# Second norm of a transformer block: products on GpSimd, full value on ScalarE, and the last output tiles one by one

## The chip, the cores and the metric

One Trainium2 chip, of which the kernel uses one core. A core has TensorE (PE: matmuls; PEld is its weight loads), VectorE (DVE), ScalarE (ACT), GpSimd (POOL) and SyncE (SP), which issues the DMAs. The engines run their own instruction lists in order and wait for each other by semaphores. The metric is the device time of one execution in microseconds (us).

## The reference

A block of width 1024 over 256 tokens in float32: an adaLN modulation from a vector c, a norm, one wide projection, causal attention of 8 heads beside a spatial gating unit, a merge, an output projection, and then the part that matters here: a second norm and a feed-forward layer of width 4096, each with a residual, and a final norm.

```python
h = rmsnorm(x, g_ffn[l]) * (1 + scale2) + shift2
x = x + gate2 * (jnp.square(jax.nn.relu(h @ w_ff1[l])) @ w_ff2[l])
return rmsnorm(x, g_final)
```

with `rmsnorm(x, g) = x * rsqrt(mean(x*x) + EPS) * g`.

## The kernel before

Everything is held transposed, features on the 128 partitions and the 256 tokens along a row, so a 1024 x 256 activation is eight tiles (ft 0 to 7) of 128 x 256. Each float32 product is made of three matmuls (`mm3`, line 70): a weight tile is rounded by ScalarE to a high part (`whi`, `high`, line 240) and VectorE forms the rest (`wlo`, `low`, line 249); an activation has a high part (`nh`, `fh`) and a low part (`nl`, `fl`) in the same way; high x high, high x low and low x high are added up in PSUM.

The feed-forward layer runs over 16 units of 256 hidden features. For units 0 to 2 the first product (`ff1`, line 619) works on the unnormalised x, so that TensorE need not wait for the norm; the roots of the second norm are multiplied in afterwards (`relu2`, line 630). From unit 3 on the product is `wide` (line 404) with the normalised activation `nh`, `nl`, which `full` (line 653) makes once for all eight tiles, tile by tile: x times the roots (`xb`, line 657), the rounded high part `nh` (line 658), the full value in place of the product (line 659), and the difference `nl` (line 660). `xb` comes from a pool tag with two buffers, so the product of tile ft writes the buffer of tile ft - 2 and waits until the `nl` of that tile has been read out of it. `full` is called for tiles 0 and 1, then 2 to 4, then 5 to 7 (lines 704, 708, 717). `ff2` (line 674) adds each unit's second product into four PSUM banks, two tiles to a bank.

PE, DVE and ACT are wrapped by `InOrder` (line 35): in the first and in the last part of the program instructions keep the order of the code, and from line 369 to line 728 a scheduler sets the order of each engine's list before the kernel runs. All instructions of the three wrapped engines carry line 44, so they are told apart by the tiles they write and read. GpSimd's instructions keep their own lines.

In the last part (lines 730 to 778) the last two units' second products are made for two tiles at a time (j = 0 to 3). VectorE adds the residual from PSUM (`x_sb`, line 740), ScalarE squares it (`sq3`, `sqt`), VectorE and once GpSimd (line 749) add the squares, and `yg` is x times the gain of the final norm. `turn` (line 758) transposes `yg` on TensorE, `sums` (line 118) adds the squares over the features with matmuls against ones, `rstd` (line 123) makes the roots on ScalarE (`ms`) and GpSimd (`rs`), and ScalarE and VectorE scale the result (`ys`) for four output DMAs.

Of the kernel before, what the change touches and what calls it, by code (L numbers as in the profile page):

```python
# [9 lines left out]
F32 = mybir.dt.float32  # L10
F32R = mybir.dt.float32r
BF16 = mybir.dt.bfloat16
AF = mybir.ActivationFunctionType
ALU = mybir.AluOpType
AX = mybir.AxisListType

P = 128
S = 256
D = 1024
KT = D // P  # L20
# [4 lines left out]
NU = DFF // 256  # L25
# [4 lines left out]
G_MIX, G_FFN, G_FIN, G_SGU = 48, 56, 64, 72  # L30
# [17 lines left out]
def block_kernel(ctx, tc, x, xT, cols, wsguT, bsgu, w_a1, w_1, w_a, w_m, w_f, out):  # L48
    nc = tc.nc
    PE, DVE, ACT = (InOrder(tc, e) for e in (nc.tensor, nc.vector, nc.scalar))  # L50
    const = ctx.enter_context(tc.tile_pool(name="const", bufs=1))
    act = ctx.enter_context(tc.tile_pool(name="act", bufs=1))
    wk = ctx.enter_context(tc.tile_pool(name="wk", bufs=2))
# [6 lines left out]
    def bank():  # L60
        return ps.tile([P, 512], F32, name="bank", tag="bank")
# [14 lines left out]
    cols_sb = const.tile([P, NCOL], F32, name="cols_sb")  # L76
# [8 lines left out]
    x_sb = act.tile([P, KT, S], F32, name="x_sb")  # L85
# [11 lines left out]
    def spin(n):  # L97
# [13 lines left out]
        out=maskf, in_=maskf, pattern=[[0, 2], [-1, P]], compare_op=ALU.is_ge,  # L111
# [6 lines left out]
    def sums(o, sq, first, last):  # L118
        for t in range(2):
            PE.matmul(out=o[:, t:t + 1], lhsT=sq[:, P * t:P * t + P], rhs=ones[:, 0:1], start=first and t == 0,  # L120
                      stop=last, skip_group_check=t == 1)
# [33 lines left out]
    for t in range(2):  # L155
        sq = act.tile([P, D + 1], F32, name="sq", tag=("b1", "b2")[t])
# [17 lines left out]
    gcol = const.tile([P, 2, KT], F32, name="gcol")  # L174
    pre = const.tile([P, 2, KT], F32, name="pre")
    for n, (sc, g) in enumerate(((SCALE1, G_MIX), (SCALE2, G_FFN))):
        DVE.scalar_tensor_tensor(
            out=pre[:, n], in0=cols_sb[:, sc:sc + KT], scalar=1.0, in1=cols_sb[:, g:g + KT],
            op0=ALU.add, op1=ALU.mult)
# [47 lines left out]
    parts = {}  # L227
# [52 lines left out]
    for kt in range(KT):  # L280
# [9 lines left out]
        hf = wk.tile([P, S], F32, name="hf", tag="hf", bufs=2)  # L290
        wp = [slice(2048 // np_ * i, 2048 // np_ * (i + 1)) for i in range(np_)]
        xk = xps[0][:, 0:S] if f else xn[:, kt]
        a, b = acol[:, 0, kt:kt + 1], bcol[:, 0, kt:kt + 1]
# [207 lines left out]
    sc, ex, tp, po, zo = {}, {}, {}, {}, {}  # L501
    A0, S0, TD, OD = 1, 5, 2, 3
    for n in range(10):
        j = n - A0
# [148 lines left out]
    def full(fts):  # L653
        for ft in fts:
            sc, sh = acol[:, 1, ft:ft + 1], bcol[:, 1, ft:ft + 1]
            xb = wk.tile([P, S], F32, name="xb", tag="hf", bufs=2)
            DVE.tensor_tensor(out=xb, in0=x_sb[:, ft], in1=rb2, op=ALU.mult)
            ACT.activation(out=nh[:, ft], in_=xb, func=AF.Identity, scale=sc, bias=sh)
            DVE.tensor_scalar(out=xb, in0=xb, scalar1=sc, scalar2=sh, op0=ALU.mult, op1=ALU.add)
            DVE.tensor_tensor(out=nl[:, ft], in0=xb, in1=nh[:, ft].bitcast(F32), op=ALU.subtract)  # L660

    def square(o):
# [11 lines left out]
    def ff2(n, fts, wp, a, first, last):  # L674
        wh, wl = wp
        fh, fl = a
        if not acc:
            acc.extend(bank() for _ in range(4))
        for ft in fts:
            o = acc[ft // 2][:, S * (ft % 2):S * (ft % 2) + S]  # L680
            for i in range(2):
                w = slice(1024 * i + P * ft, 1024 * i + P * ft + P)
                mm3(o, wh[:, w], wl[:, w], fh[:, i], fl[:, i], first and i == 0 and ft % 2 == 0,
                    last and i == 1, skip_group_check=ft % 2 == 1)
# [42 lines left out]

    PE.pinned = DVE.pinned = ACT.pinned = True

    sq3 = act.tile([P, 2, S], F32, name="sq3", tag="u1")  # L730
    yg = act.tile([P, KT, S], F32, name="yg", tag="b1")
    ss3 = bank()
    sqs = []
    for j in range(4):
        fts = (2 * j, 2 * j + 1)
        for n in (NU - 2, NU - 1):
            ff2(n, fts, parts[slot + n - NU + 2], a[n], False, n == NU - 1)
        sq = sq3 if j == 0 else wk.tile([P, 2, S], F32, name="sqt", tag="t512a")
        for i, ft in enumerate(fts):
            DVE.scalar_tensor_tensor(out=x_sb[:, ft], in0=acc[j][:, S * i:S * i + S], scalar=gcol[:, 1, ft:ft + 1],  # L740
                                     in1=x_sb[:, ft], op0=ALU.mult, op1=ALU.add)
            if j == 3:
                ACT.activation(out=sq[:, i], in_=x_sb[:, ft], func=AF.Square)
        if j < 3:
            ACT.activation(out=sq, in_=x_sb[:, 2 * j:2 * j + 2], func=AF.Square)
            if j:
                DVE.tensor_tensor(out=sq3, in0=sq3, in1=sq, op=ALU.add)
            if j == 2:
                nc.gpsimd.tensor_tensor(out=sq3[:, 0], in0=sq3[:, 0], in1=sq3[:, 1], op=ALU.add)
        for ft in fts:  # L750
            g = cols_sb[:, G_FIN + ft:G_FIN + ft + 1]
            if j < 3:
                ACT.activation(out=yg[:, ft], in_=x_sb[:, ft], func=AF.Copy, scale=g)
            else:
                DVE.tensor_scalar(out=yg[:, ft], in0=x_sb[:, ft], scalar1=g, scalar2=None, op0=ALU.mult)
    ob = [[bank() for _ in range(2)] for _ in range(2)]

    def turn(ft):
# [1 line left out]
            PE.transpose(out=ob[t][ft // 4][:, P * (ft % 4):P * (ft % 4) + P], in_=yg[:, ft, P * t:P * t + P],  # L760
                         identity=ident)

    for ft in range(4):
        turn(ft)
    for q, first, last in ((sq3[:, 0], True, False), (sq[:, 0], False, False), (sq[:, 1], False, True)):
        sums(ss3, q, first, last)
    for ft in range(4, KT):
        turn(ft)
    rs3 = rstd(ss3, D)
    ys = act.tile([P, 2, D], F32, name="ys", tag="b2")  # L770
# [55 lines left out]
```

## Time and profile before

| what | value |
|---|---|
| median of 3 runs | 360.38 us (360.15 to 360.8) |
| the profiled execution, its own time | 360.94 us |
| its span from first to last instruction | 359.1 us |
| TensorE busy | 347.7 us, 97% of the span |
| VectorE busy | 266.0 us, 74% |
| ScalarE busy | 206.9 us, 58% |
| GpSimd busy | 7.3 us, 2% |
| mean granted TensorE clock | 0.994 |

The spans of rows are in us from the span's start. A timeline row gives start, length, engine, line, operation, what it writes and reads, and in brackets how long the engine stood idle before it and what ended that. The lengths of neighbours on one engine overlap a little: the next instruction starts before the last one has drained. The profiled execution took 0.56 us more than the median.

### The profile page before, as it was taken

Reading aid. Unit: us, or ns where it says so; the run is one execution under the profiler, and the core shown is the slowest. Engines: PE = TensorE matmul, PEld = TensorE weight load, DVE = VectorE, ACT = ScalarE, POOL = GpSimd, SP = SyncE. Lnnn points to the kernel's source line nnn. Section 1 sums busy time; section 2 is a strip of 40 time slices with the busy share of each in tenths; the row PEclk is TensorE's granted clock in tenths of the full one; section 3 lists DMA queues with packets and bytes.
Section 4 is the critical chain, followed back from the end, with each engine's and each line's share of the span. In section 5 each row is a group of like instructions: output and inputs, shape, how many; then the busy total and the mean of one; then the engine's idle time right before and its main releaser. Section 6 shows DMA issues by size and latency. Waiting matters only on the chain.

```text
span 359.1 us, 6908 instructions
## 1 busy us (share of the span) xinstructions
PE 347.7 (97%) x2898; PEld 336.3 (94%) x2898; DVE 266.0 (74%) x388; ACT 206.9 (58%) x290; POOL 7.3 (2%) x16
## 2 busy tenths in 40 slices
PE   6999999999999999999999999999999999999993
PEld 5788989998999999999999999999999999999993
DVE  4898986689799989899879976866657645546343
ACT  5867679898964554546477653544534544435142
POOL 3000000000000000000000000000000000000001
PEclk9999999999999999999999999999999999999997
DMA  7999999699899897667735475774857554500003
GB/s 249 417 411 412 410 400 420 227 361 332 341 319 364 330 334 276 234 234 266 291 149 205 149 290 195 303 266 153 300 215 274 232 215 145 229 2 0 2 0 117
DMA packets 16270, 90.39 MB, mean 252 GB/s; under 512 B 1904, under 2 KB 2416, under 8 KB 7152
## 3 DMA queue, kind: packets, MB, share of 16 engines
q1 hardware_dynamic: 16240, 89.97, 66.7%
q8 instruction: 22, 0.36, 0.4%
q14 instruction: 8, 0.07, 0.0%
HBM read 88.91 MB, written 1.05 MB: 251 GB/s over the span
## 4 chain that ended last, share of the span: by engine, by line
PE 74%; ACT 8%; DVE 6%; DMA 6%; issue 2%; SPq 1%; POOL 0%; POOLq 0%; DVEq 0%; ACTq 0%
PE bank L44 74%; DVE wlo L44 3%; DMA raw<-in_w 3%; DMA raw<-in_w_a 3%; ACT whi L44 2%; ACT pr L44 2%; ACT L44 1%; DVE xb L44 1%; SPq L67 1%; ACT vs_sb L44 1%; DVE nl L44 1%; ACT r L44 1%; DVE r L44 0%; ACT v_sb L44 0%; DVE x_sb L44 0%
## 5 line engine op out<-in xcount | busy, mean ns | idle before, releaser
L44 DVE TENSOR_TENSOR wlo<-raw,whi 128x2048 fp32r<-128x2048 f32 (+2 forms) x80 | 135.8, 1712 | 44.6 <-issue 31.4
L44 ACT CAST whi<-raw 128x2048 fp32r<-128x2048 f32 (+2 forms) x74 | 113.1, 1539 | 94.6 <-PE bank L44 84.5
L44 PE MATMUL bank<-fh,whi 128*128 128x256 f32 x256 | 70.7, 276 | 0.0
L44 PE MATMUL bank<-fh,wlo 128*128 128x256 f32 x256 | 70.7, 276 | 0.0
L44 PE MATMUL bank<-fl,whi 128*128 128x256 f32 x256 | 70.7, 276 | 0.0
L44 PE MATMUL bank<-nl,whi 128*128 128x256 f32 x208 | 57.6, 277 | 0.6 <-DVE nl L44 0.6
L44 DVE SCALAR_TENSOR_TENSOR junk<-raw,csb 128x1024 bf16<-128x1024 f32 x48 | 57.4, 1219 | 0.4 <-DMA raw<-in_w_a 0.4
L44 PE MATMUL bank<-nh,whi 128*128 128x256 f32 x208 | 57.4, 276 | 0.0
L44 PE MATMUL bank<-nh,wlo 128*128 128x256 f32 x208 | 57.4, 276 | 0.0
L44 PE MATMUL bank<-hh,whi 128*128 128x256 f32 x224 | 54.9, 285 | 1.0 <-ACT hh L44 0.8
L44 PE MATMUL bank<-hl,whi 128*128 128x256 f32 x224 | 53.9, 280 | 0.3 <-DVE hl L44 0.3
L44 PE MATMUL bank<-hh,wlo 128*128 128x256 f32 x224 | 53.8, 279 | 0.0
L44 PEld LDWEIGHTS bank<-fh,wlo 128*128 128x128 f32 x256 | 48.1, 188 | 0.0
L44 PEld LDWEIGHTS bank<-fh,whi 128*128 128x128 f32 x256 | 48.1, 188 | 0.0
L44 PEld LDWEIGHTS bank<-fl,whi 128*128 128x128 f32 x256 | 48.0, 188 | 0.0
L44 PEld LDWEIGHTS bank<-hh,whi 128*128 128x128 f32 x224 | 38.8, 189 | 3.7 <-ACT hh L44 2.1
L44 PEld LDWEIGHTS bank<-nl,whi 128*128 128x128 f32 x208 | 39.0, 188 | 0.8 <-DVE nl L44 0.8
L44 PEld LDWEIGHTS bank<-nh,whi 128*128 128x128 f32 x208 | 39.0, 188 | 0.0
L44 PEld LDWEIGHTS bank<-nh,wlo 128*128 128x128 f32 x208 | 39.0, 188 | 0.0
L44 PEld LDWEIGHTS bank<-hl,whi 128*128 128x128 f32 x224 | 38.3, 189 | 0.6 <-DVE hl L44 0.5
L44 PEld LDWEIGHTS bank<-hh,wlo 128*128 128x128 f32 x224 | 38.1, 188 | 0.1
L44 DVE TENSOR_TENSOR fl<-r,fh 128x512 fp32r<-128x512 f32 x16 | 11.1, 691 | 20.4 <-PE bank L44 20.1
(156 smaller groups left out, 538.1 us busy)
## 6 DMA issues: line engine op xcount, KB each, us to landing
raw<-in_w_f SPq DMA_DIRECT2D x32, 1024.0 KB, 4.8
raw<-in_w_a SPq DMA_DIRECT2D x22, 1024.0 KB, 7.3
raw<-in_w_m SPq DMA_DIRECT2D x16, 1024.0 KB, 7.3
raw<-in_w SPq DMA_DIRECT2D x12, 512.0 KB, 9.6
raw<-in_w_a SPq DMA_DIRECT2D x4, 512.0 KB, 7.2
raw<-in_w SPq DMA_DIRECT2D x8, 256.0 KB, 7.5
xt<-in_x SPq DMA_DIRECT2D x2, 512.0 KB, 3.8
raw<-in_w_m SPq DMA_DIRECT2D x4, 256.0 KB, 6.3
```

The source lines that it names most:

```text
L44: return lambda *a, **k: pin(op(*a, **k))
L67: nc.sync.dma_start(out=t[:, n * i:n * i + n], in_=src[:, n * i:n * i + n])
```

## The change

In `full` the product x times the roots goes from VectorE to GpSimd, and the full value goes from VectorE to ScalarE, which leaves VectorE the subtraction alone. `full` serves all eight tiles. In the last part the products of tiles 4 to 7 are made one tile at a time, in the order 4, 6, 5, 7; every tile is squared by itself, VectorE adds the squares tile by tile, the addition on GpSimd goes away, only the very last tile's square is summed by itself on TensorE, and `yg` of all tiles but the last is made by ScalarE.

```diff
--- before.py
+++ after.py
@@ -654,9 +654,9 @@
         for ft in fts:
             sc, sh = acol[:, 1, ft:ft + 1], bcol[:, 1, ft:ft + 1]
             xb = wk.tile([P, S], F32, name="xb", tag="hf", bufs=2)
-            DVE.tensor_tensor(out=xb, in0=x_sb[:, ft], in1=rb2, op=ALU.mult)
+            nc.gpsimd.tensor_tensor(out=xb, in0=x_sb[:, ft], in1=rb2, op=ALU.mult)
             ACT.activation(out=nh[:, ft], in_=xb, func=AF.Identity, scale=sc, bias=sh)
-            DVE.tensor_scalar(out=xb, in0=xb, scalar1=sc, scalar2=sh, op0=ALU.mult, op1=ALU.add)
+            ACT.activation(out=xb, in_=xb, func=AF.Identity, scale=sc, bias=sh)
             DVE.tensor_tensor(out=nl[:, ft], in0=xb, in1=nh[:, ft].bitcast(F32), op=ALU.subtract)
 
     def square(o):
@@ -727,32 +727,36 @@
 
     PE.pinned = DVE.pinned = ACT.pinned = True
 
-    sq3 = act.tile([P, 2, S], F32, name="sq3", tag="u1")
+    sq3 = act.tile([P, S], F32, name="sq3", tag="u1")
     yg = act.tile([P, KT, S], F32, name="yg", tag="b1")
+
+    last_of = (0, 1, 2, 3, 4, 6, 5, 7)
+    sq_of = {}
+
+    def add_square(k):
+        if k > 0:
+            DVE.tensor_tensor(out=sq3, in0=sq3, in1=sq_of.pop(k), op=ALU.add)
+
+    for k, ft in enumerate(last_of):
+        fts = (ft, ft + 1) if k < 4 else (ft,)
+        if k % 2 == 0 or k >= 4:
+            for n in (NU - 2, NU - 1):
+                ff2(n, fts, parts[slot + n - NU + 2], a[n], False, n == NU - 1)
+        if k == KT - 1:
+            add_square(k - 1)
+        x = x_sb[:, ft]
+        DVE.scalar_tensor_tensor(out=x, in0=acc[ft // 2][:, S * (ft % 2):S * (ft % 2) + S],
+                                 scalar=gcol[:, 1, ft:ft + 1], in1=x, op0=ALU.mult, op1=ALU.add)
+        if 0 < k < KT - 1:
+            add_square(k - 1)
+        sq_of[k] = sq3 if k == 0 else wk.tile([P, S], F32, name="sqt", tag="hf")
+        ACT.activation(out=sq_of[k], in_=x, func=AF.Square)
+        g = cols_sb[:, G_FIN + ft:G_FIN + ft + 1]
+        if k < KT - 1:
+            ACT.activation(out=yg[:, ft], in_=x, func=AF.Copy, scale=g)
+        else:
+            DVE.tensor_scalar(out=yg[:, ft], in0=x, scalar1=g, scalar2=None, op0=ALU.mult)
     ss3 = bank()
-    sqs = []
-    for j in range(4):
-        fts = (2 * j, 2 * j + 1)
-        for n in (NU - 2, NU - 1):
-            ff2(n, fts, parts[slot + n - NU + 2], a[n], False, n == NU - 1)
-        sq = sq3 if j == 0 else wk.tile([P, 2, S], F32, name="sqt", tag="t512a")
-        for i, ft in enumerate(fts):
-            DVE.scalar_tensor_tensor(out=x_sb[:, ft], in0=acc[j][:, S * i:S * i + S], scalar=gcol[:, 1, ft:ft + 1],
-                                     in1=x_sb[:, ft], op0=ALU.mult, op1=ALU.add)
-            if j == 3:
-                ACT.activation(out=sq[:, i], in_=x_sb[:, ft], func=AF.Square)
-        if j < 3:
-            ACT.activation(out=sq, in_=x_sb[:, 2 * j:2 * j + 2], func=AF.Square)
-            if j:
-                DVE.tensor_tensor(out=sq3, in0=sq3, in1=sq, op=ALU.add)
-            if j == 2:
-                nc.gpsimd.tensor_tensor(out=sq3[:, 0], in0=sq3[:, 0], in1=sq3[:, 1], op=ALU.add)
-        for ft in fts:
-            g = cols_sb[:, G_FIN + ft:G_FIN + ft + 1]
-            if j < 3:
-                ACT.activation(out=yg[:, ft], in_=x_sb[:, ft], func=AF.Copy, scale=g)
-            else:
-                DVE.tensor_scalar(out=yg[:, ft], in0=x_sb[:, ft], scalar1=g, scalar2=None, op0=ALU.mult)
     ob = [[bank() for _ in range(2)] for _ in range(2)]
 
     def turn(ft):
@@ -760,11 +764,11 @@
             PE.transpose(out=ob[t][ft // 4][:, P * (ft % 4):P * (ft % 4) + P], in_=yg[:, ft, P * t:P * t + P],
                          identity=ident)
 
-    for ft in range(4):
+    for ft in last_of[0:3]:
         turn(ft)
-    for q, first, last in ((sq3[:, 0], True, False), (sq[:, 0], False, False), (sq[:, 1], False, True)):
-        sums(ss3, q, first, last)
-    for ft in range(4, KT):
+    sums(ss3, sq3, True, False)
+    sums(ss3, sq_of[KT - 1], False, True)
+    for ft in last_of[3:]:
         turn(ft)
     rs3 = rstd(ss3, D)
     ys = act.tile([P, 2, D], F32, name="ys", tag="b2")
```

The code leaves open what the scheduler makes of it between lines 369 and 728. Three places of the engines' lists follow; in their names `xb_2467`, `xb_2472` and `xb_2477` belong to tiles 5, 6 and 7, `xb_2402` to tile 4, `whi_2411` is the rounded weight of the next second product, `whi_2316` and `wlo_2494` the parts of the weight of the next `wide`, and `junk_2559` is a dot product of the modulation.

ScalarE, where tiles 5 and 6 are normalised, before:

```order
L44 ACTIVATE nh_2173<-xb_2467,bcol_187,acol_186 128x256 [waits DVE_49]
L44 CAST whi_2411<-raw_2409 128x2048 [waits DMAHW7_49,PE_49]
L44 ACTIVATE nh_2173<-xb_2472,bcol_187,acol_186 128x256 [waits DVE_49]
L44 ACTIVATE r_2482<-r_2482,bw_2483 128x256
L44 ACTIVATE r2_2484<-r_2482 128x512 [waits Activation_49]
```

and with the change:

```order
L44 ACTIVATE nh_2173<-xb_2467,bcol_187,acol_186 128x256 [waits Pool_49]
L44 ACTIVATE nh_2173<-xb_2472,bcol_187,acol_186 128x256 [waits Pool_49]
L44 CAST whi_2411<-raw_2409 128x2048 [waits DMAHW7_49,PE_49]
L44 ACTIVATE xb_2467<-xb_2467,bcol_187,acol_186 128x256 [waits DVE_49,Activation_49]
L44 ACTIVATE xb_2472<-xb_2472,bcol_187,acol_186 128x256 [waits DVE_49,Activation_49]
L44 ACTIVATE r_2482<-r_2482,bw_2483 128x256
```

The high parts of tiles 5 and 6 now stand together ahead of the cast, wait for GpSimd, and the full values of both tiles stand behind the cast.

VectorE at the same tiles, before:

```order
L44 TENSOR_SCALAR xb_2467<-xb_2467,acol_186,bcol_187 128x256 [waits Activation_49]
L44 TENSOR_TENSOR xb_2472<-x_sb_87,rb2_2172 128x256 [waits DVE_49]
L44 TENSOR_TENSOR nl_2174<-xb_2467,nh_2173 128x256 [waits DVE_49]
L44 TENSOR_TENSOR wlo_2494<-raw_2314,whi_2316 128x2048 [waits DMAHW6_49,PE_49]
L44 TENSOR_SCALAR xb_2472<-xb_2472,acol_186,bcol_187 128x256 [waits Activation_49]
L44 TENSOR_TENSOR xb_2477<-x_sb_87,rb2_2172 128x256 [waits DVE_49]
L44 TENSOR_TENSOR nl_2174<-xb_2472,nh_2173 128x256 [waits DVE_49]
```

and with the change:

```order
L44 TENSOR_TENSOR nl_2174<-xb_2402,nh_2173 128x256 [waits Activation_49]
L44 TENSOR_TENSOR wlo_2494<-raw_2314,whi_2316 128x2048 [waits DMAHW6_49,PE_49]
L44 TENSOR_TENSOR nl_2174<-xb_2467,nh_2173 128x256 [waits Activation_49]
L44 TENSOR_TENSOR nl_2174<-xb_2472,nh_2173 128x256 [waits Activation_49]
L44 SCALAR_TENSOR_TENSOR junk_2559,acc_2560<-raw_2240,csb_127 128x1024 [waits DMAHW4_49,DVE_49]
L44 TENSOR_TENSOR nl_2174<-xb_2477,nh_2173 128x256 [waits Activation_49]
```

The long `wlo_2494` stood behind the `nl` of tile 5 and now stands directly behind that of tile 4; earlier in the new list `wlo_2312` stands directly behind the `nl` of tile 0 and `wlo_2407` directly behind that of tile 2.

GpSimd, whose list had nothing between the two roots, with the change:

```order
L127 TENSOR_TENSOR rs_2236<-ms_2234,nhalf_108 128x2 [waits Activation_49]
...
L657 TENSOR_TENSOR xb_2397<-x_sb_87,rb2_2172 128x256 [waits DVE_49]
L657 TENSOR_TENSOR xb_2402<-x_sb_87,rb2_2172 128x256 [waits DVE_49]
L657 TENSOR_TENSOR xb_2467<-x_sb_87,rb2_2172 128x256 [waits DVE_49]
L657 TENSOR_TENSOR xb_2472<-x_sb_87,rb2_2172 128x256 [waits DVE_49]
L657 TENSOR_TENSOR xb_2477<-x_sb_87,rb2_2172 128x256 [waits DVE_49]
```

From tile 2 on, each of these products waits for VectorE's `nl` of the tile two before it.

## Rows read from the trace of the kernel before

**Rows 1.** The page, busy time of each engine in the span.

```profile
PE 347.7 (97%) x2898; PEld 336.3 (94%) x2898; DVE 266.0 (74%) x388; ACT 206.9 (58%) x290; POOL 7.3 (2%) x16
```

**Rows 2.** TensorE's waits over the span: us in total, times, longest.

```profile
PE bank L44 <- DVE nl L44: 0.6, 1, 0.6
```

**Rows 3.** Timeline of TensorE at tiles 5 and 6 of the first wide unit.

```profile
200.06 0.28 PE L44 MATMUL bank<-nl,whi 128*128 128x256 f32 x1
...
200.63 0.28 PE L44 MATMUL bank<-nh,whi 128*128 128x256 f32 x1
201.55 0.39 PE L44 MATMUL bank<-nl,whi 128*128 128x256 f32 x1 [0.65 <-DVE nl L44]
```

**Rows 4.** Groups of VectorE from 182.6 to 204.5: busy us, mean ns, idle before.

```profile
L44 DVE TENSOR_TENSOR nl<-xb,nh 128x256 fp32r<-128x256 f32 x8 | 3.4, 419 | 0.0
L44 DVE TENSOR_SCALAR xb<-xb,acol,bcol 128x256 f32<-128x256 f32 x8 | 3.3, 410 | 0.5 <-ACT nh L44 0.5
L44 DVE TENSOR_TENSOR xb<-x_sb,rb 128x256 f32<-128x256 f32 x8 | 3.2, 418 | 0.0
L44 DVE SCALAR_TENSOR_TENSOR junk<-raw,csb 128x1024 bf16<-128x1024 f32 x1 | 1.2, 1222 | 0.0
```

**Rows 5.** Groups of ScalarE from 182.6 to 202, same columns.

```profile
L44 ACT CAST whi<-raw 128x2048 fp32r<-128x2048 f32 x3 | 5.7, 1899 | 0.0
L44 ACT ACTIVATE nh<-xb,bcol,acol 128x256 fp32r<-128x256 f32 x8 | 4.8, 596 | 1.6 <-DVE xb L44 1.6
L44 ACT ACTIVATE r<-r,bw 128x256 f32<-128x256 f32 x6 | 2.9, 505 | 1.0 <-DVE r L44 0.9
L44 ACT CAST fh<-r 128x512 fp32r<-128x512 f32 x3 | 1.9, 617 | 0.1
```

**Rows 6.** Timeline of ScalarE at the roots and around the cast whi_2411.

```profile
182.65 0.37 ACT L44 COPY rb<-bank 128x256 f32<-128x256 f32 x1 [1.81 <-PE bank L44]
...
197.09 1.90 ACT L44 CAST whi<-raw 128x2048 fp32r<-128x2048 f32 x1
198.89 0.60 ACT L44 ACTIVATE nh<-xb,bcol,acol 128x256 fp32r<-128x256 f32 x1
```

**Rows 7.** Timeline of GpSimd over the span.

```profile
7.26 0.91 POOL L158 TENSOR_TENSOR rs<-ms,nhalf 128x1 f32<-128x1 f32 x1 [0.72 <-ACT sq L44]
64.45 0.70 POOL L535 TENSOR_TENSOR vrs<-vms,nhalf 128x2 f32<-128x2 f32 x1 [56.29 <-DVE vms L44]
80.57 1.10 POOL L519 TENSOR_SCALAR_AFFINE_SELECT wsg<-wsg 128x1024 f32<-128x1024 f32 x1 [15.42 <-DMA wsg<-in_wsguT]
180.92 0.81 POOL L127 TENSOR_TENSOR rs<-ms,nhalf 128x2 f32<-128x2 f32 x1 [99.26 <-ACT ms L44]
349.82 0.73 POOL L749 TENSOR_TENSOR sq<-sq 128x256 f32<-128x256 f32 x1 [168.08 <-DVE sq L44]
```

**Rows 8.** Timeline of VectorE beside three of the GpSimd rows above.

```profile
7.39 0.74 DVE L44 TENSOR_SCALAR xt<-xt,rs 128x1024 f32<-128x1024 f32 x1
...
80.64 3.17 DVE L44 TENSOR_TENSOR wlo<-raw,whi 128x2048 fp32r<-128x2048 f32 x1 [1.06 <-ACT whi L44]
...
178.89 2.29 DVE L44 TENSOR_TENSOR wlo<-raw,whi 128x2048 fp32r<-128x2048 f32 x1 [0.20 <-PE bank L44]
```

**Rows 9.** View by tile, wlo: duration ns min/median/max, first and last start, forms.

```profile
L44 DVE TENSOR_TENSOR wlo<-raw,whi x80: 682/2283/3170, 12.6 to 333.9; 128x2048 fp32r<-128x2048 f32 x48, 128x512 fp32r<-128x512 f32 x24, 128x1024 fp32r<-128x1024 f32 x8
```

**Rows 10.** Timelines of VectorE, ScalarE, TensorE and ScalarE at the end.

```profile
350.14 0.88 DVE L44 SCALAR_TENSOR_TENSOR x_sb<-bank,gcol,x_sb 128x256 f32<-128x256 f32 x2 [0.40 <-PE bank L44]
...
350.71 0.75 ACT L44 ACTIVATE sqt<-x_sb 128x256 f32<-128x256 f32 x2 [0.90 <-DVE x_sb L44]
...
351.18 1.05 PE L44 MATMUL bank<-ones,sqt 128*128 128x1 f32 x8
...
352.27 0.26 ACT L44 ACTIVATE ms<-bank,eps 128x2 f32<-128x2 f32 x1 [0.81 <-PE bank L44]
```

**Rows 11.** Windows from 353 to 359: busy, granted clock, DMA share, GB/s.

```profile
353.00:359.00 6.00, 0.17 (x2) 0.00 (x0) 1.41 (x2) 1.26 (x2) 0.32 (x1) 0.63 0.47 175
```

## The prediction

> **What bounds the kernel now.** I read the busy times first, then TensorE's waits, then the timelines of the two places that the diff touches. TensorE is busy 97% of the span [rows 1], so only its idle time and the end after its last product can be won or lost. Of its waits one falls into the second norm: 0.6 us for an `nl` [rows 2]. The timeline shows the place: inside the first `wide` unit, at the `nl` of tile 6, two matmuls start 0.92 us apart [rows 3], where others start 0.11 us apart (200.06 to 200.63 is five of them). So the norm costs 0.8 us now. The reason is VectorE: its 24 pieces of the norm (8 products, 8 full values, 8 `nl`) take 3.2 + 3.3 + 3.4 us there, with no idle time before most of them [rows 4]. ScalarE has 1.6 us of idle time before its `nh` [rows 5]. The other place is the end: a last pair of residuals on VectorE, two squares on ScalarE, the sums on TensorE, then `ms` and the roots.
>
> **Moved work, by the piece.** VectorE loses 8 products of 0.418 us and 8 full values of 0.410 us, 6.6 us [rows 4]. ScalarE gains 8 full values; the nearest row is `nh`, the same operation with the same operands, 0.596 us [rows 5]. ScalarE starts its next instruction about 0.1 us before the last ends (a cast of 1.90 us has its follower 1.80 us later [rows 6]), so each adds 0.5 us, 4.0 us in all. GpSimd gains 8 products. The nearest row is its addition of 128 x 256 values, two inputs, 0.73 us [rows 7]; I take that, with VectorE's 0.42 as the lower and GpSimd's 0.91 as the upper bound. None of this is TensorE's work, so by busy time alone it would be free. What counts is when the `nl` of tiles 5, 6 and 7 are ready, because TensorE wants that of tile 5 at 200.06 [rows 3] and has no other work listed ahead of it.
>
> **The chain without any quarrel between engines.** The roots are there at 183.0 [rows 6]; GpSimd's first product ends at 183.8. From 183.9 ScalarE works off 16 instructions without a wait: three `nh` and three full values (0.5 each), four `r` (0.41), two `fh` and two squares of the same size (0.52), two casts (1.80) [rows 5], 10.3 us, to 194.2. The third full value among them ends at 192.0, the third `nl` at 192.4, and GpSimd's product of tile 4, which waits for that `nl` because there are two buffers, at 193.3. The full values of tiles 3 and 4 end at 195.8 and 196.3, their `nl` at 196.3 and 196.8, the products of tiles 5 and 6 at 197.1 and 197.8. Now the moved order bites: the `nh` of tile 6 waits until 197.8, the cast behind it takes ScalarE until 200.2, and only then comes the full value of tile 5, to 200.7, and its `nl`, to 201.2. TensorE loses 1.1 us there, and about 1.4 us more at tile 7, whose product waits for the `nl` of tile 5. That is 2.5 us against 0.8 us now: 1.7 us slower.
>
> **What the two engines do to each other.** VectorE's 48 subtractions of 128 x 2048 take 2.28 us in the median [rows 9], like that at 178.89; the longest started at 80.64 beside a GpSimd instruction of 1.10 us and took 3.17 us [rows 7, 8]: 0.88 us longer, about what was left of the other's time. The other way round is seen on smaller instructions: GpSimd's roots take 0.70 us with VectorE at rest, 0.81 us when they start 0.26 us before a subtraction ends, and 0.91 us when VectorE scales `xt` meanwhile, ending 0.04 us after it [rows 7, 8]. I read this as: an operation of one waits until the other's is over. The addition at 349.82 kept its 0.73 us although the residual, which reads one input from PSUM, began at 350.14 [rows 7, 10], so I take such operations as harmless. No row shows a GpSimd product behind a whole 2.28 us subtraction, so its cost there lies between nothing and all of it; I take all, since both rows at hand show a wait to the other's end.
>
> The Trainium skill ("SBUF — State Buffer", section "Who interferes with whom") says the same more sharply: a VectorE instruction with two SBUF inputs and a GpSimd instruction that reads SBUF exclude each other, and whichever comes second is blocked for the whole of the first. By that rule the sum is the next paragraph's; were it wrong for long subtractions, the sum would be the last one's.
>
> **The chain with it.** Each `nl` that GpSimd waits for at tiles 0, 2 and 4 has a `wlo` directly behind it on VectorE, so GpSimd asks just after the long subtraction has begun. At tile 0 that costs nothing, since its product is wanted only 2 us later. After the `nl` of tile 2 `wlo_2407` (192.4 to 194.7) and the `fl` behind it hold VectorE to 195.2; the product of tile 4 ends at 196.0, the full values of tiles 3 and 4 at 197.1 and 197.6. The products of tiles 5 and 6 meet `wlo_2494`: the second surely stands behind it and ends at 201.7, whichever of the first and the `nl` of tile 4, which become ready at the same time, goes first. Then `nh` of tile 6 to 202.4, the cast to 204.2, the full value of tile 5 to 204.7, its `nl` to 205.2. TensorE, which wanted it at 200.06, stands for 5.1 us. After that a second tie decides: if the product of tile 7 comes ahead of the `nl` of tile 6, TensorE loses 0.5 and 0.8 us more, together 6.4; if it comes behind that and the dot product (1.22 us [rows 4]), 1.8 and 1.2 us more, together 8.1. Less the 0.8 us of now: 5.6 to 7.3 us slower. ScalarE's queue behind the waiting `nh` holds the cast and both full values; VectorE's behind the waiting `nl` holds the dot product and `wlo_2549`, and the weights' DMAs wait for those `wlo`; all are late by what TensorE is late, so no further wait opens.
>
> **The end.** The last tile is alone in its square. Now two squares (0.75 us from 350.71) and eight passes of TensorE (1.05 us from 351.18) stand ahead of `ms` at 352.27 [rows 10]. With the change one square ends at 351.1, four passes take 0.6 us, `ms` can start at 351.8: 0.5 us earlier. Bounds: nothing, and the 0.81 us that ScalarE waits there [rows 10]. The extra additions on VectorE, 7 of some 0.4 us, fall into its waits for TensorE (0.40 us before the last residual [rows 10]), and the addition taken from GpSimd, 0.73 us, ran beside TensorE's products: both count as nothing; without that cover the last addition would delay the last residual by 0.4 us. Tile 5 writes a bank that VectorE is still reading for tile 4, but the 12 matmuls of tile 6 (1.4 us) lie between: nothing.
>
> **Sum.** +5.6 to +7.3 us, -0.5 us: 5.1 to 6.8, in the middle 5.9, since two ties are undecided. The profiled execution took 360.94 us, the median is 360.38; on the median that is 366.3 us (365.5 to 367.2).
>
> **Rivals.** *No blocking:* GpSimd's products run freely. For it: no row shows a GpSimd product stopped by a long subtraction. Against: the longer instructions [rows 7, 8]. Price 1.7 - 0.5: 361.6 us; with GpSimd at 0.42 us about 360.4, at 0.91 us 362.4. *The clock falls:* TensorE stands for some 5 us; after its last work the granted clock of the six microseconds from 353 is 0.63 [rows 11], so its lower level of 1.2 GHz sets in within that time. Half speed for as long as the stand costs half of 5.1 us: 2.5 us, 368.8. Against: nowhere in the trace does it stand so long between products. The Trainium skill ("TensorE: Matmul & The Clock Gate", "What's actually happening") also has the engine fall to 1.2 GHz when idle and return when busy. *Faster:* VectorE, rid of 6.6 us, has each `nl` ready in time, the 0.8 us wait goes and the end gains 0.5: 359.1 us. It decides at one point, the `nl` of tile 5 before 200.06; by the chain above it is 1.1 us late even without blocking, so GpSimd would have to take under about 0.35 us a product. That the change does not reach the machine can't be: the engines' lists show it.
>
> **Chances.** Blocking 0.63, blocking with the lower clock 0.10, no blocking 0.21, faster 0.06. A measurement of this kernel can tell 0.2%, 0.7 us, from no change; 0.07 of the free case lies within that (a short GpSimd product). So slower 0.87, same 0.07, faster 0.06. The range, 361.2 to 368.0 us, leaves out the faster case, the cheap part of the free one and most of the clock's: 2 in 10. The likeliest case's own range is 365.5 to 367.2.
>
> **What would show it.** Right: GpSimd products of tiles 4 and 6 of 2 to 3 us, or starting only where a `wlo` ends; a TensorE wait of about 5 us on `nl` near 200 to 205; `ms` 1.7 us, not 2.1, after the last residual begins. Wrong: all eight products near 0.73 us; a wait of 1 us; or the wait gone, and a shorter time.

## The result, and the profile after

The changed kernel takes 364.34 us in the median, the one before 360.26 us beside it on the same chip: 1.0111 times as long, 95% interval 1.0092 to 1.0131. Forecast were 366.3 us and slower; the direction and the range (361.2 to 368.0) held, the likeliest case's own range (365.5 to 367.2) did not. Some executions of every kernel here, the one before included, take 5 to 8 us longer than the rest; the ratios leave these out, and where a median holds many of them I go by the ratio. The change's other four took 363.45, 363.61 and 363.66 us at a mean granted clock of 0.992, and 365.02 us at 0.985.

The profiled execution took 363.61 us, its span is 361.9 us. TensorE's waits in it, the line that answers to [rows 2]:

```profile
PE bank L44 <- DVE nl L44: 4.2, 2, 3.8
```

The 0.6 us of before have become two waits, one of 3.8 us. TensorE's timeline shows them, at the `nl` of tile 5 (of tile 6 in [rows 3]) and at that of tile 7, and its last product:

```profile
202.22 0.39 PE L44 MATMUL bank<-nl,whi 128*128 128x256 f32 x1 [3.80 <-DVE nl L44]
...
205.42 0.58 PE L44 MATMUL bank<-nl,whi 128*128 128x256 f32 x1 [0.35 <-DVE nl L44]
...
353.04 0.28 PE L44 MATMUL bank<-fh,wlo 128*128 128x256 f32 x1
```

Follow it back. GpSimd's timeline has the eight products:

```profile
181.29 1.44 POOL L657 TENSOR_TENSOR xb<-x_sb,rb 128x256 f32<-128x256 f32 x2 [1.36 <-ACT rb L44]
184.50 2.72 POOL L657 TENSOR_TENSOR xb<-x_sb,rb 128x256 f32<-128x256 f32 x1 [1.77 <-DVE nl L44]
188.74 0.74 POOL L657 TENSOR_TENSOR xb<-x_sb,rb 128x256 f32<-128x256 f32 x1 [1.51 <-DVE nl L44]
190.65 2.72 POOL L657 TENSOR_TENSOR xb<-x_sb,rb 128x256 f32<-128x256 f32 x1 [1.17 <-DVE nl L44]
195.03 3.75 POOL L657 TENSOR_TENSOR xb<-x_sb,rb 128x256 f32<-128x256 f32 x2 [1.67 <-DVE nl L44]
202.25 1.01 POOL L657 TENSOR_TENSOR xb<-x_sb,rb 128x256 f32<-128x256 f32 x1 [3.46 <-DVE nl L44]
```

Free, a product takes 0.72 to 0.74 us (the first two, and that of tile 3). Those of tiles 2 and 4 take 2.72 us. VectorE's timeline says why:

```profile
190.49 2.28 DVE L44 TENSOR_TENSOR wlo<-raw,whi 128x2048 fp32r<-128x2048 f32 x1
192.69 1.23 DVE L44 TENSOR_TENSOR fl<-r,fh 128x512 fp32r<-128x512 f32 x1
...
194.53 0.92 DVE L44 TENSOR_TENSOR nl<-xb,nh 128x256 fp32r<-128x256 f32 x2 [0.21 <-ACT xb L44]
195.37 2.83 DVE L44 TENSOR_TENSOR wlo<-raw,whi 128x2048 fp32r<-128x2048 f32 x1
201.74 0.92 DVE L44 TENSOR_TENSOR nl<-xb,nh 128x256 fp32r<-128x256 f32 x2 [3.54 <-ACT xb L44]
202.58 1.76 DVE L44 SCALAR_TENSOR_TENSOR junk<-raw,csb 128x1024 bf16<-128x1024 f32 x1
```

The product of tile 4 is asked for at 190.65, just after `wlo_2407` began at 190.49; that ends at 192.77 and the product at 193.37, 0.60 us later. Then `fl`, normally about 0.69 us, waits in its turn and takes 1.23 us. Two products (tiles 5 and 6) share the stretch from 195.03 to 198.78 with `wlo_2494`, which is stretched from 2.28 to 2.83 us. ScalarE's timeline carries the delay on:

```profile
196.09 0.60 ACT L44 ACTIVATE nh<-xb,bcol,acol 128x256 fp32r<-128x256 f32 x1 [0.70 <-POOL xb L657]
198.82 0.60 ACT L44 ACTIVATE nh<-xb,bcol,acol 128x256 fp32r<-128x256 f32 x1 [2.13 <-POOL xb L657]
199.32 1.88 ACT L44 CAST whi<-raw 128x2048 fp32r<-128x2048 f32 x1
201.11 1.09 ACT L44 ACTIVATE xb<-xb,bcol,acol 128x256 f32<-128x256 f32 x2
...
203.29 0.60 ACT L44 ACTIVATE nh<-xb,bcol,acol 128x256 fp32r<-128x256 f32 x1 [0.69 <-POOL xb L657]
```

The `nh` of tile 6 stands 2.13 us for its product; the cast behind it needs nothing of it, yet waits too, and behind the cast stands the full value of tile 5, whose `nl` TensorE wants. In [rows 6] that cast began at 197.09 without waiting.

The clock fell as well. Windows of TensorE (length, busy us with its instructions, granted clock, DMA share, GB/s):

```profile
199.00:202.00 3.00, 0.00 (x0) 1.00 0.82 317
202.00:203.00 1.00, 0.78 (x6) 0.93 0.24 98
203.00:206.00 3.00, 2.65 (x12) 0.50 0.00 0
206.00:207.00 1.00, 1.00 (x9) 0.86 0.00 0
```

After the stand the granted clock is 0.50 from 203 to 206, that is 1.2 GHz; matmuls then start 0.21 us apart instead of 0.11.

At the end, VectorE's last residual and ScalarE's `ms`, two timelines, as in [rows 10]:

```profile
353.43 0.48 DVE L44 SCALAR_TENSOR_TENSOR x_sb<-bank,gcol,x_sb 128x256 f32<-128x256 f32 x1
...
355.12 0.26 ACT L44 ACTIVATE ms<-bank,eps 128x2 f32<-128x2 f32 x1 [0.70 <-PE bank L44]
```

`ms` begins 1.69 us after the last residual. Before, 2.13 us are counted from the first residual of a pair (two in 0.88 us [rows 10]); counted from the second, which by that length began about 0.40 us later, it was some 1.7 us too. The gain shows from the start of the last product on: `ms` comes 2.08 us after it (353.04 to 355.12) in place of 2.46 us (349.81 to 352.27).

For the account I need two more rows of the kernel before, the `nl` of tile 7 and the last product on TensorE's timeline:

```profile
204.01 0.33 PE L44 MATMUL bank<-nl,whi 128*128 128x256 f32 x1
...
349.81 0.28 PE L44 MATMUL bank<-fh,wlo 128*128 128x256 f32 x1
```

The profile after reached the roots (`rb`) at 180.85, the one before at 182.65 [rows 6]; the part ahead of them is not touched, so I count from `rb`:

| us from the start of `rb` | before | after | predicted |
|---|---|---|---|
| product of tile 4 ends (GpSimd) | | 12.52 | 13.35 |
| product of tile 6 ends (GpSimd) | | 17.93 | 19.05 |
| first matmul with `nl` of tile 5 | 17.41 | 21.37 | 22.55 |
| first matmul with `nl` of tile 7 | 21.36 | 24.57 | |
| last product starts | 167.16 | 172.19 | |
| from there to the span's end | 9.29 | 8.86 | 0.5 less |

So the norm lost 5.03 us and the end gave back 0.43, 4.6 us in these two executions; by the ratio the loss is 4.0 us (3.3 to 4.7). The `nl` of tile 7 is 3.21 us late and stands twelve matmuls further ahead in TensorE's order than before (1.36 us at 0.113 each): 4.57 us. The other 0.46 us falls behind that `nl`, where the first matmuls still run at the low clock.

### The profile page after: what moved, and what is told of

It is laid out like the page before. It is cut to its first block, busy times and chain, and to the rows that moved or that the text cites. A ratio compares the mean times of both kernels' runs of the same rounds, so it can differ in the third digit from the quotient of the medians.

```text
span 361.9 us, 6928 instructions
## 1 busy us (share of the span) xinstructions
PE 347.9 (96%) x2894; PEld 336.0 (93%) x2894; DVE 262.8 (73%) x375; ACT 211.3 (58%) x302; POOL 20.7 (6%) x23
## 4 chain that ended last, share of the span: by engine, by line
PE 43%; issue 43%; ACT 4%; DMA 4%; DVE 3%; POOL 2%; POOLq 0%; DVEq 0%; SPq 0%; ACTq 0%
PE bank L44 43%; DMA raw<-in_w 3%; POOL xb L657 2%; ACT whi L44 1%; DVE wlo L44 1%; DVE junk L44 1%; ACT r L44 1%; ACT xb L44 1%; DMA cols_sb<-in_cols 0%; ACT nh L44 0%; DVE yg L44 0%; DVE fl L44 0%; DVE nl L44 0%; DVE ys L44 0%; DVE xt L44 0%
```

## Experiments

My theory was a loop: with two buffers a product waits for the `nl` of two tiles before, GpSimd then stands behind a `wlo`, and the `nh` that waits for GpSimd holds ScalarE's cast and the full values behind it. The rivals were ScalarE's added work, blocking alone, and the clock.

**The end alone** (the norm as before, the new last part).

```diff
-            nc.gpsimd.tensor_tensor(out=xb, in0=x_sb[:, ft], in1=rb2, op=ALU.mult)
+            DVE.tensor_tensor(out=xb, in0=x_sb[:, ft], in1=rb2, op=ALU.mult)
...
-            ACT.activation(out=xb, in_=xb, func=AF.Identity, scale=sc, bias=sh)
+            DVE.tensor_scalar(out=xb, in0=xb, scalar1=sc, scalar2=sh, op0=ALU.mult, op1=ALU.add)
```

> The second norm as before, only the new last part. If the changed trace is read rightly, the last part alone is worth -0.4 us (from the last product to the end 8.9 us in place of 9.3) and the norm all of the loss: -0.4 us against before, ratio 0.999. If single tiles cost TensorE waits for VectorE at the shared banks, 0 to +1 us.

Measured: 359.36 us against 359.76, ratio 0.9984 (0.9967 to 1.0002). From the last product to the end of the span 8.78 us instead of 9.29. As expected in the trace, at the edge of what the ratio can tell.

**The norm alone** (the new `full`, the old last part; this edit is against the kernel before, all others are against the change).

```diff
-            DVE.tensor_tensor(out=xb, in0=x_sb[:, ft], in1=rb2, op=ALU.mult)
+            nc.gpsimd.tensor_tensor(out=xb, in0=x_sb[:, ft], in1=rb2, op=ALU.mult)
...
-            DVE.tensor_scalar(out=xb, in0=xb, scalar1=sc, scalar2=sh, op0=ALU.mult, op1=ALU.add)
+            ACT.activation(out=xb, in_=xb, func=AF.Identity, scale=sc, bias=sh)
```

> The new second norm, the last part as before. Parts that add up: +4.8 us against before (4.4 + 0.4), with the TensorE wait on nl of 3.8 us and some 3.4 us at the lower clock unchanged. Less than +4 would mean that the two edits hinder each other.

Measured: ratio 1.0194 (1.0130 to 1.0258), profiled execution 364.81 us. Its times scatter (364.81, 365.03, 366.43 and 369.41 us), so the interval is wide; the expected 4.8 us lie at its lower end. The stand is the same 3.79 us, but the clock stayed low until 207.5, and from `rb` to the last product it is 172.88 us, 0.69 more than with the whole change. The loss is the norm's.

**Five buffers.**

```diff
-            xb = wk.tile([P, S], F32, name="xb", tag="hf", bufs=2)
+            xb = wk.tile([P, S], F32, name="xb", tag="hf", bufs=5)
```

> The change, with five buffers in place of two for the products (the tag is shared with other tiles, which get them too). Theory A: the loss comes from GpSimd's product waiting for the nl of two tiles before, right behind which a long subtraction holds VectorE and GpSimd apart. Then the products are all made early, tile 5's nl is ready before TensorE wants it, the clock stays up: -1.3 to 0 us against before. Theory B: ScalarE, with 4 us more to do, is the bound whatever the buffers: the wait on nl stays at 2 us or more and the time at +2 us or more.

Measured: 358.69 us, ratio 0.9988 (0.9971 to 1.0005). GpSimd's last product, and TensorE's only wait for an `nl`, on their timelines:

```profile
190.83 2.72 POOL L657 TENSOR_TENSOR xb<-x_sb,rb 128x256 f32<-128x256 f32 x1 [1.16 <-DVE nl L44]
```

```profile
200.28 0.38 PE L44 MATMUL bank<-nl,whi 128*128 128x256 f32 x1 [0.42 <-DVE nl L44]
```

A product still loses 2 us to a `wlo`, yet TensorE's wait is 0.42 us, less than the 0.65 us of before [rows 3]: neither blocking nor ScalarE's eight extra instructions cost time where there is room to run ahead. One thing went along: the scheduler now puts the full value of tile 5 ahead of the cast. The run with the right cast, below, moves the cast alone.

**Keeping TensorE busy in the stand** (zeros multiplied into the running sum).

```diff
+            if ko == 4:
+                for _ in range(fill):
+                    PE.matmul(out=o[:, 0:S], lhsT=zeros[:, 0:P], rhs=zeros, start=False, stop=False)
...
-            f[n + 3] = wide(slot, nh, nl, KT)
+            f[n + 3] = wide(slot, nh, nl, KT, 0, 32 if n == 0 else 0)
```

> The change, with 32 matmuls of zeros added into the same bank ahead of tile 5 of the first wide unit, so that TensorE works while it waits for nl (some 3.5 us of work into a 3.8 us wait). If the lower clock after the wait costs 1.5 us (15 matmuls at 0.21 in place of 0.11 us), the granted clock stays at 1.00 and the time is 1 to 1.6 us below the change: +2.8 to +3.4 us against before. If the clock falls for another reason, or costs nothing on the path, +4.4 us or more.

Measured: 363.88 us, ratio 1.0127 (1.0106 to 1.0148): no gain. The clock did stay at its upper level (1.00 in the windows from 199 to 207), but a wait took its place (timeline of TensorE):

```profile
203.19 0.38 PE L44 MATMUL bank<-nl,whi 128*128 128x256 f32 x1 [0.29 <-DVE nl L44]
...
206.39 0.39 PE L44 MATMUL bank<-nl,whi 128*128 128x256 f32 x1 [1.09 <-DVE nl L44]
```

Here `rb` began at 181.82, so the matmul with the `nl` of tile 7 starts at 24.57 us from it, to the hundredth as with the change. In the change TensorE, most of the time at half clock, merely filled with 14 matmuls the time until that `nl` was there. From `rb` to the last product it is 172.03 us against 172.19. The two orders differ by two matmuls: a pair `fh`, `fl` stands ahead of that `nl` in the change and behind it here (first its row in the change, then here):

```profile
204.44 0.41 PE L44 MATMUL bank<-fh,whi 128*128 128x256 f32 x1
...
207.09 0.28 PE L44 MATMUL bank<-fh,whi 128*128 128x256 f32 x1
```

Two matmuls at 0.113 us are 0.23 us, so the low clock cost the change's profiled execution some 0.2 to 0.4 us, not the 1.5 us that I had counted from its slow matmuls.

**The long subtractions in quarters.**

```diff
+            cut = 4 if NM + 3 <= n <= NM + 6 else pieces(n)
-            m = 2048 // pieces(n)
-            for i in range(pieces(n)):
+            m = 2048 // cut
+            for i in range(cut):
```

> The change, with the four subtractions wlo of 128x2048 around the second norm cut into four of 128x512 each; every engine's order stays as it is, and the ring keeps its two buffers. Theory: a waiting GpSimd product gets its turn at the end of the VectorE instruction that runs, not at the end of those queued behind it; then no product takes over 1.4 us (a quarter of 2.28 us, 0.57, and its own 0.73) where the change's took 2.72, the products of tiles 4 to 6 end 1.4 to 3 us sooner, and TensorE stands at nl of tile 5 for 0.5 to 2 us instead of 3.8, too short for the clock to fall. Time: 1 to 2.5 us over the kernel before (the change: 4.1 by medians). Rival: the turn goes to VectorE's next instruction while VectorE has one ready: products of 2.7 us as before, stand 3.8 us or more, 4 us or more over the kernel before.

Measured: 362.7 us, ratio 1.0087 (1.0069 to 1.0106). GpSimd's timeline and TensorE's:

```profile
184.40 1.21 POOL L658 TENSOR_TENSOR xb<-x_sb,rb 128x256 f32<-128x256 f32 x1 [1.78 <-DVE nl L44]
...
191.18 1.12 POOL L658 TENSOR_TENSOR xb<-x_sb,rb 128x256 f32<-128x256 f32 x1 [1.17 <-DVE nl L44]
195.47 2.00 POOL L658 TENSOR_TENSOR xb<-x_sb,rb 128x256 f32<-128x256 f32 x2 [3.17 <-DVE nl L44]
```

```profile
200.91 0.38 PE L44 MATMUL bank<-nl,whi 128*128 128x256 f32 x1 [2.29 <-DVE nl L44]
```

No product takes over 1.21 us: the turn goes to the waiting engine at the end of one instruction, not of those queued behind. The `nl` of tile 5 comes 1.2 us sooner (20.17 us after `rb` at 180.74), so blocking behind whole subtractions is about a third of the stand; 2.3 us are left with it cut short, and the time, 3.1 us over the kernel before by the ratio, is a little above what I expected. The stand was not too short for the clock either: in the profiled execution it fell (the last section shows it). That execution took 364.24 us, the other five 362.48 to 362.92.

**A copy in place of the product** (one input from SBUF).

```diff
-            nc.gpsimd.tensor_tensor(out=xb, in0=x_sb[:, ft], in1=rb2, op=ALU.mult)
+            nc.gpsimd.tensor_copy(out=xb, in_=rb2)
```

> The change, with GpSimd's product replaced by a copy of the roots rb into xb (one input from SBUF in place of two; leaves out the product with x_sb); the order is the same on every engine. Theory A: any GpSimd instruction that reads SBUF waits for a VectorE instruction with two inputs there: a free copy takes 0.4 to 0.75 us, those that fall beside wlo still take 2.3 to 2.8 us, the stand is 3.3 to 4 us, and the time is 3.5 to 4.5 us over the kernel before. Theory B: only two inputs on both sides exclude each other: no copy over 0.8 us, the stand at most 1.5 us, the time 0 to 1.5 us over the kernel before (the prediction's case without blocking gave 1.2).

Measured: 361.91 us, ratio 1.0065 (1.0045 to 1.0084). GpSimd's timeline:

```profile
188.45 0.40 POOL L657 COPY xb<-rb 128x256 f32<-128x256 f32 x1 [1.84 <-DVE nl L44]
190.36 2.40 POOL L657 COPY xb<-rb 128x256 f32<-128x256 f32 x1 [1.51 <-DVE nl L44]
```

The durations are theory A's: the number of GpSimd's inputs does not matter. The time is neither's: the stand was 2.52 us, the `nl` of tile 5 1.28 us sooner than in the change (20.09 us after `rb`). A copy is 0.33 us shorter than a product; those of tiles 0, 2, 4 and 6 follow one another in the loop, which makes 1.3 us. I had left that out of A's time.

**The full value on ScalarE alone, and the product on GpSimd alone** (two buffers each).

```diff
-            nc.gpsimd.tensor_tensor(out=xb, in0=x_sb[:, ft], in1=rb2, op=ALU.mult)
+            DVE.tensor_tensor(out=xb, in0=x_sb[:, ft], in1=rb2, op=ALU.mult)
```

> The change with the product put back on VectorE: nothing on GpSimd, the full value on ScalarE, two buffers. Does ScalarE's part cost by itself? Theory (ring and blocking together make the loss): without blocking the product of tile 4 takes 0.42 us on VectorE, but it still waits for nl of tile 2 and the full value waits behind ScalarE's cast whi of 1.9 us: a stand of 0.5 to 2.5 us at nl, the time 0 to 2 us over the kernel before. Rival (ScalarE's eight added instructions of 0.6 us are what is too much): a stand of 3.5 us or more, 3.5 us or more over the kernel before.

```diff
-            ACT.activation(out=xb, in_=xb, func=AF.Identity, scale=sc, bias=sh)
+            DVE.tensor_scalar(out=xb, in0=xb, scalar1=sc, scalar2=sh, op0=ALU.mult, op1=ALU.add)
```

> The change with the full value put back on VectorE: only the product is on GpSimd, two buffers. Theory: products are still held by wlo up to 2.7 us, but the full value no longer passes ScalarE, so a buffer comes free 1 to 3 us sooner and the product runs ahead of its need: TensorE waits at most 1 us for nl, the time 0.5 us under to 1 us over the kernel before. Rival (blocking alone makes the loss, wherever the full value is): a stand of 3 us or more, 3 us or more over the kernel before.

Measured: 1.0025 (0.9981 to 1.0069) and 0.9987 (0.9957 to 1.0016). The only waits of TensorE for an `nl` in the first and in the second of them:

```profile
200.88 0.38 PE L44 MATMUL bank<-nl,whi 128*128 128x256 f32 x1 [0.39 <-DVE nl L44]
```

```profile
201.17 0.39 PE L44 MATMUL bank<-nl,whi 128*128 128x256 f32 x1 [1.01 <-DVE nl L44]
```

Either half of the change costs little or nothing by itself (the first interval is wide). The loss came only with both halves, and with the ring of two. The scheduler's orders changed along with the halves: with the full value alone, for one, the `nh` of tile 6 stands behind the full value of tile 5, no longer ahead of the cast.

**Buffers of their own for tiles 5 to 7.**

```diff
-            xb = wk.tile([P, S], F32, name="xb", tag="hf", bufs=2)
+            xb = wk.tile([P, S], F32, name="xb", tag="xb" if ft > 4 else "hf", bufs=3 if ft > 4 else 2)
```

> The change with three buffers of their own for tiles 5 to 7; tiles 0 to 4 keep the ring of two. So the products of tiles 2 to 4 still wait for nl and stand behind wlo, those of tiles 5 to 7 don't. The order of every engine is that of the run with five buffers. Theory (the late turns of the ring carry the loss, the first ones are early enough): products of tiles 2 and 4 still up to 2.7 us, TensorE waits at most 1 us for nl, the time 0.7 us under to 0.7 us over the kernel before. Rival (the delay that the product of tile 4 takes from wlo carries half of it): a stand of 1.5 to 2.5 us, 1.5 to 2.5 us over the kernel before.

Measured: 359.93 us, ratio 0.9999 (0.9979 to 1.0018). My expectation was wrong on GpSimd's list: the scheduler put the products of tiles 5 to 7 ahead of those of tiles 2 to 4. TensorE's timeline:

```profile
199.63 0.39 PE L44 MATMUL bank<-nl,whi 128*128 128x256 f32 x1 [0.29 <-DVE nl L44]
...
201.02 0.39 PE L44 MATMUL bank<-nl,whi 128*128 128x256 f32 x1 [0.41 <-DVE nl L44]
```

The product of tile 4, again 2.72 us long, ends 12.87 us after `rb` (180.85), no sooner than in the change, and the stand is gone: what costs is the late turn of the ring, the products of tiles 5 and 6 and what stands behind them. The cast, here too behind the full value of tile 5, is not told apart from that.

**The cast written later.**

```diff
-        high(n + 2)
+        if n + 2 != 24:
+            high(n + 2)
...
             full(range(5, KT))
+            high(24)
```

> The change with the cast whi_2411 of the next weights written behind the second norm's last tiles, so that on ScalarE the full values of tiles 5 and 6 go ahead of it; the ring keeps two buffers and the product stays on GpSimd (the order around it shifts: on VectorE nl of tiles 3 to 6 go ahead of the subtraction wlo_2494). Theory (the ring loses because a full value stands behind a cast and the next product behind a subtraction): a stand of 0 to 1.5 us in all at nl, the time 0.5 us under to 1.5 us over the kernel before. Rival (a ring of two through three engines is too slow in any order): a stand of 3 us or more, 3 us or more over the kernel before.

Measured: 363.38 us, ratio 1.0093 (1.0064 to 1.0122). I had taken the wrong cast: 24 is `whi_2316`, which `wlo_2494` needs, not `whi_2411`. So `wlo_2494` came late and the order around it with it; tile 5 cost TensorE 0.42 us, tile 7 0.79 us at its `nh` and 1.67 us at its `nl`, which stood behind `wlo_2494`. Of the expectation this settles nothing.

**The right cast behind the full values.**

```diff
-        high(n + 2)
+        if n + 2 != 25:
+            high(n + 2)
...
             full(range(5, KT))
+            high(25)
```

> The change with the cast that stands behind the nh of tile 6 on ScalarE (whi_2411) put behind the full values of tiles 5 and 6; every other place in the orders of all engines stays. (The run called The cast written later moved another cast, that of the weight that wlo_2494 needs.) Theory, from the rows of the change: nh of tile 6 ends at 199.4, so the full value of tile 5 ends at 199.9 in place of 201.7, its nl at 200.4: a stand of 1.8 to 2.2 us at tile 5 in place of 3.8. But the nh of tile 7 now stands behind the cast, so its nl comes only 0.5 to 0.8 us sooner than in the change; TensorE waits 1 to 2 us for it, and the time is 3 to 3.9 us over the kernel before (the change: 4.1 by medians). Rival (the cast between nh and full value is what makes the loss): a stand of 2 us in all, the time 0.5 to 2 us over the kernel before.

Measured: 365.03 us against 359.65, ratio 1.0148 (1.0128 to 1.0167). TensorE's timeline, and its clock in windows:

```profile
202.07 0.38 PE L44 MATMUL bank<-nl,whi 128*128 128x256 f32 x1 [2.00 <-DVE nl L44]
...
204.79 0.58 PE L44 MATMUL bank<-nh,whi 128*128 128x256 f32 x1 [1.16 <-ACT nh L44]
206.26 0.58 PE L44 MATMUL bank<-nl,whi 128*128 128x256 f32 x1 [0.46 <-DVE nl L44]
```

```profile
205.00:207.00 2.00, 1.54 (x6) 0.50 0.00 0
207.00:209.00 2.00, 2.00 (x12) 0.50 0.00 0
```

The waits are the theory's to a tenth: 2.00 us at tile 5, 1.6 at tile 7, and the `nl` of tile 7 at 23.77 us after `rb` (182.49), 0.8 us sooner than in the change. So the cast was half of the stand at tile 5, and moving it sends most of that on to tile 7. The time is not the theory's: it is longer than the change's. From the `nl` of tile 7 to the last product (355.82) it takes 149.56 us, where the change took 147.62 and the filled kernel, with two matmuls more behind that `nl`, 147.46: here the low clock lies behind the last wait, nothing absorbs it, and it costs some 2 us.

**Product on GpSimd, full value on VectorE, five buffers, the new end.**

```diff
-            xb = wk.tile([P, S], F32, name="xb", tag="hf", bufs=2)
+            xb = wk.tile([P, S], F32, name="xb", tag="hf", bufs=5)
...
-            ACT.activation(out=xb, in_=xb, func=AF.Identity, scale=sc, bias=sh)
+            DVE.tensor_scalar(out=xb, in0=xb, scalar1=sc, scalar2=sh, op0=ALU.mult, op1=ALU.add)
```

> What the runs so far point to: the product on GpSimd, the full value on VectorE as in the kernel before, five buffers, and the change's last part. Theory: no wait for nl left (the kernel before loses 0.65 us there) and 0.4 us less at the end: 1.2 to 0.5 us under the kernel before. Rival: GpSimd's products hold up VectorE's wlo and fl enough to cost what they save: within 0.3 us of the kernel before or slower.

Measured: 358.83 us against 360.11, ratio 0.9962 (0.9940 to 0.9984): 0.4% under the kernel before, and so under the change. TensorE waits for no `nl` any more.

## Why the prediction came out as it did

- **The place and the mechanism held.** TensorE stands at the `nl` of tile 5, behind the full value, the cast, the `nh` of tile 6 and a product that stood behind `wlo_2494`. Three of the predicted signs are there: a GpSimd product of 2.72 us at tile 4 (that of tile 6 shares 3.75 us with tile 5's), a wait of several us near 200 to 205, `ms` at 1.7 us. The last tells less than I meant, since the 2.1 us beside it count from the first residual of a pair. That the time lies in the stated range says little either: the range, 6.8 us wide, also holds the 361.6 us of the case without blocking. It is the rows that tell the two apart.
- **GpSimd's price held:** taken 0.73 us, measured 0.72 to 0.74. **The end held:** predicted 0.5 us, measured 0.43 in the trace of the change and 0.51 with the end alone.
- **The term that was mis-sized is "`wlo_2407` and the `fl` behind it hold VectorE to 195.2; the product of tile 4 ends at 196.0".** I let VectorE finish both before GpSimd got its turn. In fact GpSimd, waiting, goes next, and `fl` waits (1.23 us). And the product ends 0.60 us after the subtraction, where I had added the whole 0.73. That of tile 4 ended 0.83 us sooner after `rb` than predicted, that of tile 6 1.12 us, and the stand was 3.8 us, not 5.1. The quarters show the same rule: a turn at every instruction's end.
- **The ties.** At tile 7 a way between my two came: GpSimd's product (asked for at 202.25, 1.01 us) waited for the `nl` of tile 6 and went ahead of the dot product, which took 1.76 in place of 1.22 us. Predicted were 5.6 to 7.3 us net of today's wait; measured 5.03.
- **The clock.** I gave "blocking with the lower clock" 0.10 and 2.5 us. The clock did fall to 1.2 GHz, for some 3 us instead of 5, and cost 0.2 to 0.4 us in the profiled execution, since the wait at tile 7 covered most of it. The execution at a mean clock of 0.985 took some 1.4 us more; it has no trace, so where its clock was low is not shown. The rival was right in what happens and wrong in its price here: slow matmuls ahead of a wait cost only what that wait does not absorb. Where they lay behind the last wait they did cost about 2 us. The Trainium skill ("TensorE: Matmul & The Clock Gate", "What's actually happening") has the engine drop when idle; the trace agrees (0.50 after the stand), but not each time, see below.
- **What I had not seen** is how little takes the loss away: three more buffers for the last tiles, or one half of the change less. The prediction took blocking for the cause (chance 0.63, against 0.21 without it); the runs show it as about a third of the stand at tile 5, the cast as about half when moved by itself, and neither is the whole, since the ring hands a delay on to tile 7. Whether five buffers help with the cast still ahead of the full value of tile 5 was not tried: in both kernels with more buffers and the whole change the scheduler moved that too.

## What to carry to other kernels

Before moving a step to an engine with time to spare, count the turns that its buffers let it run ahead: through three engines and two buffers every queue on the way (a cast, a long subtraction) enters the loop, and with five buffers, in the order that the scheduler then chose, the same move cost nothing measurable. A low clock costs only what the next wait does not absorb, so ask where the last wait lies. For engines that exclude each other, reckon that the waiting one goes next, at the end of the running instruction.

## What the runs showed of the hardware

**The exclusion works both ways, with two inputs on GpSimd's side or one.** Beside one 2.28 us subtraction a product went from 0.74 to 2.72 us and a copy from 0.40 to 2.40; beside a product `fl` went from 0.69 to 1.23 us. The Trainium skill ("SBUF — State Buffer", "Who interferes with whom") names two-input VectorE instructions against a GpSimd instruction that reads SBUF; the copy agrees. It also lets a VectorE instruction with one input take part in certain modes. The fastest kernel shows such a pair, the full value on VectorE and a product, on two timelines:

```profile
190.41 0.75 DVE L44 TENSOR_TENSOR nl<-xb,nh 128x256 fp32r<-128x256 f32 x2
191.08 0.83 DVE L44 TENSOR_SCALAR xb<-xb,acol,bcol 128x256 f32<-128x256 f32 x1
...
190.90 0.86 POOL L657 TENSOR_TENSOR xb<-x_sb,rb 128x256 f32<-128x256 f32 x1 [1.61 <-DVE nl L44]
```

The full value, 0.41 us when free, took 0.83 us beside the product. The product's 0.86 us, against 0.74 when free, show nothing of that pair: the second `nl` ahead, with two inputs, ended at 191.16, and the product 0.60 us later, as behind the subtraction.

**The stand's length alone does not decide the clock.** With the copies TensorE stood 2.52 us and the clock stayed; with the quarters it stood 2.29 us and the clock fell. Windows of the first and of the second:

```profile
201.00:203.00 2.00, 1.93 (x14) 1.00 0.23 94
203.00:207.00 4.00, 3.42 (x30) 1.00 0.00 0
```

```profile
201.00:203.00 2.00, 1.88 (x12) 0.80 0.86 365
203.00:207.00 4.00, 3.54 (x16) 0.50 0.11 47
```

Even the same stand ends in different ways. In the change (3.80 us) the clock was 1.00 through the stand and fell after it; with the norm alone (3.79 us) it fell within it, a window in which no matmul ran:

```profile
200.00:202.00 2.00, 0.00 (x0) 0.71 1.01 426
```

What else decides it, these runs do not show. So a low clock's price taken from one execution need not hold for the next.
